# Gated DeltaNet and RWKV-7 step: the convolution's small PSUM copies on another engine, and the gate columns' transposes at another place

## The chip, the cores and the metric

The kernel runs on one core of one Trainium2 chip. The metric is the device time of one execution in microseconds (us); lower is better. The profile shows five engines: TensorE (PE for its matmuls, PEld for its weight loads), VectorE (DVE), ScalarE (ACT), GpSimd (POOL) and SyncE (SP), which issues the DMAs. Each engine works through its own queue in order; an instruction that waits for a semaphore holds up everything behind it on that engine, and nothing on the others.

## The reference

The program is one inference step of two layers, for 1040 prompt tokens (16 of them learned) and 8 samples of 8 tokens: 1104 tokens of width 1024. The first layer is a gated DeltaNet, and only it is touched:

```python
proj = xn @ w_in
qkv, z, b, a = proj[..., :c1], proj[..., c1:c2], proj[..., c2:c3], proj[..., c3:]
qkv, new_buf = causal_conv(qkv, conv_buf, conv_w)   # width 4, SiLU; new_buf: the last 3 rows before it
beta = jax.nn.sigmoid(b)
g = -jnp.exp(a_log) * jax.nn.softplus(a + dt_bias)  # then cumulative sums, exponentials, a triangular solve
```

There are 8 query/key heads and 16 value heads of 128 channels, hence 32 channel tiles (8 of queries, 8 of keys, 16 of values) that go through the convolution, and 16 tiles of output gates z that do not. The convolution begins with the last three rows of each sample's past (the history, an input), and the last three rows of each sequence are an output. The second layer is an RWKV-7 mixer, followed by a final norm.

## The kernel before

Tokens lie along the free dimension in three segments of 384, 384 and 336; the 64 sample tokens come first. A dense product of one 128-channel tile is 3 segments of 24 fp32 matmuls, since activations and weights are split into a high and a low part (`dense`, tile names d, dk, dq, dv, dz; ScalarE makes the high weights whi, GpSimd the low ones wlo).

`layer0` computes the two gates' rows first (`gates`): a dense product of the 32 gate channels, then on VectorE and ScalarE a chain of operations over 16 rows of 1104 tokens, which ends with the tile rows (lines 367 to 378). Rows are stored to DRAM (drow, line 389), and nine 128-token pieces of rows are transposed by TensorE into PSUM, three to a bank (lines 390 to 393). From there VectorE and ScalarE fill gcol, the same gates as columns with tokens on partitions (lines 396 to 399). gcol scales almost everything that follows.

Then come eight rounds of one key head and its two value heads. In each round: `gdn_keys` (convolution of the key tile), `gdn_prep` (scores of keys with keys, decay factors E read from drow, a masked exponential with a column of gcol as bias, and the inverse of the triangular blocks: 62 dependent VectorE operations invtmp and invT, lines 470 and 472, then a round through DRAM to the tiles T1n and TT), `gdn_queries`, `gdn_values` (two value tiles), `gdn_gate` (two tiles of z) and `gdn_recur`, the recurrence over nine token tiles, in which TensorE's rA products, ScalarE's w and VectorE's X and S alternate. In the first round `gdn_gate` comes ahead of `gdn_prep`.

`conv_tile` is the convolution of one tile and is called 32 times. For each it loads the history (24 rows of 128 channels), transposes it with TensorE (fhist), and copies the 24 columns from PSUM into the ends of the first segment's eight sample stretches (line 418, VectorE). ScalarE copies the dense products into raw (lines 420, 421, 426), scales by the first tap, VectorE adds three taps (cvy, line 434), ScalarE takes tanh, and VectorE multiplies (line 438). GpSimd collects the last three rows of each sequence in last. At the end TensorE transposes them (flast), VectorE copies 27 rows of 128 from PSUM to lasts (line 452), and two DMAs store them.

fhist, flast, the columns' transposes, the key scores and the values' transposes share two PSUM banks (tag f); the dense products of this layer use two others (tag d). In the first layer no order is written out by hand. The program text gives priorities and data dependences; from these a list scheduler, which goes by its own estimate of each instruction's time, draws up the queue of every engine when the program is built, and gives out the buffers as they come free in that estimate. So the order in the trace is not the order of the text, and a moved instruction can change the order of others. In the second layer the order on TensorE is written out by hand.

The views name a helper's line for some operations: line 73 is `transpose`, line 76 `mm`, line 62 `act`.

Of the kernel before, what the change touches and what calls it, by code (L numbers as in the profile page):

```python
# [35 lines left out]
class Builder:  # L36
# [307 lines left out]
    def gates(self, xh, xl):  # L344
        nc, i, t, gp = self.nc, self.i, self.t, self.gatep
        al, wz, rows, g, sm = self.gate_in
        nea = t(gp, [128, 1], "nea")
        self.act(nea[32:48], al[32:48, 0:1], AF.Exp)
        nc.vector.tensor_scalar(nea[32:48], nea[32:48], -1.0, None, op0=ALU.mult)
        whi = t(gp, [128, 8, 64], "whi2", dt=F32R)  # L350
        wlo = t(gp, [128, 8, 64], "wlo2", dt=F32R)
        self.split(wz, whi, wlo)
        w = ([whi[:, 0:4, :], whi[:, 4:8, :]], [wlo[:, 0:4, :], wlo[:, 4:8, :]])
        x = t(gp, [48, NT], "ax")
        y = t(gp, [48, NT], "ay")
        for s, (c0, n) in enumerate(SEGS):
            p = self.dense(w, 64, xh, xl, s)
            b = rows[0:16, c0:c0 + n]
            self.act(b, p[0:16, 0:n], AF.Tanh, scale=0.5)
            nc.vector.tensor_scalar(b, b, 0.5, 0.5, op0=ALU.mult, op1=ALU.add)  # L360
            xa, ya = x[32:48, c0:c0 + n], y[32:48, c0:c0 + n]
            self.act(xa, p[32:48, 0:n], AF.Identity, bias=al[32:48, 1:2])
            nc.vector.scalar_tensor_tensor(ya, xa, -1.0, xa, op0=ALU.mult, op1=ALU.max)
            self.act(ya, ya, AF.Exp, scale=-1.0)
        xa, ya = x[32:48], y[32:48]
        self.act(ya, ya, AF.Ln, bias=1.0)
        nc.vector.scalar_tensor_tensor(ya, xa, 0.0, ya, op0=ALU.max, op1=ALU.add)
        nc.vector.tensor_scalar(g[32:48, 0:NT], ya, nea[32:48], None, op0=ALU.mult)
        gc = rows[32:48]
        nc.vector.tensor_tensor_scan(gc, sm[32:48], g[32:48], 0.0, op0=ALU.mult, op1=ALU.add)  # L370
        gd = rows[64:80]
        c3 = lambda x: x.rearrange("p (c k) -> p c k", k=128)
        c8 = lambda x: x[:, 0:64].rearrange("p (c k) -> p c k", k=8)
        v, v8 = c3(gc), c8(gc)
        nc.vector.tensor_tensor(c3(gd)[:, 1:9], v[:, 1:9, 127:128].broadcast_to([16, 8, 128]), v[:, 1:9], op=ALU.subtract)
        nc.vector.tensor_tensor(c3(gd)[:, 0:1, 64:128], v[:, 0:1, 127:128].broadcast_to([16, 1, 64]), v[:, 0:1, 64:128],
                                op=ALU.subtract)
        nc.vector.tensor_tensor(c8(gd), v8[:, :, 7:8].broadcast_to([16, 8, 8]), v8, op=ALU.subtract)
        egl = t(gp, [48, 17], "egl")
        self.act(egl[32:48, 0:8].unsqueeze(2), v8[:, :, 7:8], AF.Exp)  # L380
        self.act(egl[32:48, 8:17].unsqueeze(2), v[:, :, 127:128], AF.Exp)
        dgl = self.dram([16, 17], "dgl")
        nc.sync.dma_start(dgl, egl[32:48])
        nc.sync.dma_start(self.eglb.rearrange("p h c -> p (h c)"),
                          dgl.rearrange("(o h) c -> o (h c)", o=1).broadcast_to([128, 272]))

        self.drow = self.dram([8, 9, 2, 128], "drow")
        for j in range(8):
            nc.sync.dma_start(self.drow[j].rearrange("t h k -> h t k"), c3(gc)[2 * j:2 * j + 2])
        for t3 in range(3):  # L390
            p = self.ps("f", 2)
            for k in range(3):
                self.transpose(p[:, 96 * k:96 * k + 96], rows[:, (3 * t3 + k) * 128:(3 * t3 + k + 1) * 128])
            pv = p[:, 0:288].rearrange("p (k x h) -> p k x h", k=3, h=16)
            c = self.col[:, 3 * t3:3 * t3 + 3]
            nc.vector.tensor_copy(c[:, :, 0, :], pv[:, :, 0, :])
            nc.vector.tensor_scalar(c[:, :, 1, :], pv[:, :, 2, :], -1.0, None, op0=ALU.mult)
            self.act(c[:, :, 2, :], pv[:, :, 2, :], AF.Exp)
            self.act(c[:, :, 3, :], pv[:, :, 4, :], AF.Exp)


    def conv_tile(self, ft, xh, xl, dst, done=None):

        nc, i, t = self.nc, self.i, self.t
        w, self.wnext = self.wnext or self.load_w(i["gdn_w_in"][0][:, ft * 128:(ft + 1) * 128]), None
        hist = t(self.fp, [24, 128], "hist", 1)
        nc.sync.dma_start(hist, i["state_gdn_conv"][0].rearrange("b r c -> (b r) c")[:, ft * 128:(ft + 1) * 128])
        last = t(self.fp, [128, 27], "last", 2)
        cw = [self.cw[:, k, ft:ft + 1] for k in range(4)]
        prev = None  # L410
        for s, (c0, n) in enumerate(SEGS):
            p = self.dense(w, 128, xh, xl, s, label="q" if ft < 8 else "k" if ft < 16 else "v")
            raw = t(self.fp, [128, 411], "raw", 3)
            if s == 0:
                sv = raw[:, 0:88].rearrange("p (b r) -> p b r", r=11)
                hp = self.ps("f", 2, "hist")
                self.transpose(hp[:, 0:24], hist)
                nc.vector.tensor_copy(sv[:, :, 0:3], hp[:, 0:24].rearrange("p (b r) -> p b r", r=3))
                nc.gpsimd.memset(raw[:, 88:91], 0.0)
                nc.scalar.copy(sv[:, :, 3:11], p[:, 0:64].rearrange("p (b r) -> p b r", r=8))  # L420
                nc.scalar.copy(raw[:, 91:411], p[:, 64:384])
                wd = 408
                nc.gpsimd.tensor_copy(last[:, 0:24].rearrange("p (b r) -> p b r", r=3), sv[:, :, 8:11])
            else:
                nc.gpsimd.tensor_copy(raw[:, 0:3], prev)
                nc.scalar.copy(raw[:, 3:3 + n], p[:, 0:n])
                wd = n
            prev = raw[:, wd:wd + 3]
            if s == 2:
                nc.gpsimd.tensor_copy(last[:, 24:27], prev)  # L430
            y = t(self.fp, [128, 408], "cvy", 2)
            self.act(y[:, 0:wd], raw[:, 0:wd], AF.Identity, scale=cw[0])
            for k in range(1, 4):
                nc.vector.scalar_tensor_tensor(y[:, 0:wd], raw[:, k:k + wd], cw[k], y[:, 0:wd], op0=ALU.mult, op1=ALU.add)  # L434
            e = raw
            self.act(e[:, 0:wd], y[:, 0:wd], AF.Tanh, scale=0.5)
            d = dst(s)
            silu = lambda d, e, y: nc.vector.scalar_tensor_tensor(d, e, 1.0, y, op0=ALU.add, op1=ALU.mult)
            if s == 0:
                v8 = lambda q: q[:, 0:88].rearrange("p (b r) -> p b r", r=11)[:, :, 0:8]  # L440
                silu(d[:, 0:64].rearrange("p (b r) -> p b r", r=8), v8(e), v8(y))
                silu(d[:, 64:384], e[:, 88:408], y[:, 88:408])
            else:
                silu(d[:, 0:n], e[:, 0:n], y[:, 0:n])
                if n < 384:
                    nc.gpsimd.memset(d[:, n:384], 0.0)
            if done is not None:
                done(s, d)
        lp = self.ps("f", 2, "last")
        self.transpose(lp[0:27, 0:128], last)  # L450
        ls = t(self.fp, [27, 128], "lasts", 1)
        nc.vector.tensor_copy(ls, lp[0:27, 0:128])
        nc.sync.dma_start(self.o["s_gdn_conv"][0].rearrange("b r c -> (b r) c")[:, ft * 128:(ft + 1) * 128], ls[0:24])
        nc.sync.dma_start(self.o["p_gdn_conv"][0, 0][:, ft * 128:(ft + 1) * 128], ls[24:27])

# [1365 lines left out]
    def layer0(self, top, right, xa, xc):  # L1821
        tc, nc, t = self.tc, self.nc, self.t
# [13 lines left out]
        self.vectors()  # L1836
        kh, kl = [h[:, k] for h in hi for k in range(4)], [l[:, k] for h in lo for l in h for k in range(l.shape[1])]
        rows = [xa[:, k] for k in range(6)] + [xc[:, k] for k in range(10)]
        self.gates(kh, kl)
        for j in range(8):  # L1840
            G, before = self.gdn_keys(j, kh, kl), G if j else None
            if j == 0:
                if QF:
                    self.gdn_queries(j, G, kh, kl)
                self.gdn_zero()
                gates.close()
                self.gp = pool("gdn", ctx)
                if ZF:
                    self.gdn_gate(j, G, kh, kl)
# [43 lines left out]
        lp = pool("rnorm", out, side="right")  # L1893
# [304 lines left out]
```

## Time and profile before

| | us |
|---|---|
| median of 3 runs | 2295.79 |
| lowest and highest | 2290.16, 2301.59 |
| the profiled execution | 2295.8 |
| its span | 2294.1 |
| TensorE, VectorE, ScalarE, GpSimd busy | 2133.1, 1558.2, 1273.9, 949.9 |

The span is the time from the first instruction to the last on the core; 1.7 us of the profiled execution lie around it. The rows of gates are made up to 67 us from the span's start, the eight rounds of the first layer run from about 45 to 1180 us, and the second layer fills the rest. In a timeline row stand the start, the time, engine, line, operation, the tile written and those read, and in brackets the time for which the engine had stood before and what released it. A waits row has the engine and tile that waited, the one waited for, the total in us, how often, and the longest. The granted clock (PEclk) is TensorE's clock as the throttle granted it, as a share of full speed.

### The profile page before, as it was taken

To read this page: it belongs to the slowest core of one execution; us is meant where nothing else is said; L and a number is where in the kernel's file an instruction comes from. 1 tells how busy PE (TensorE), PEld (TensorE's weight loads), DVE (VectorE), ACT (ScalarE), POOL (GpSimd) and SP (SyncE) were. 2 spreads that over 40 slices of the span, in tenths; PEclk is the share of its full clock that TensorE was granted. 3 is DMA by queue.
4 is the path that set the end of the run, shared out by engine and by line. 5 is a ranking of instruction groups with operands and counts; after the bars stand their busy time and mean duration, and the time that the engine had idled before them with its cause. 6 is when DMAs were issued, how large, how long until landed. Compare 5 with 4: busy or idle time off the path is not lost.

```text
span 2294.1 us, 55205 instructions
## 1 busy us (share of the span) xinstructions
PE 2133.1 (93%) x20452; PEld 1943.4 (85%) x20452; DVE 1558.2 (68%) x4200; ACT 1273.9 (56%) x3638; POOL 949.9 (41%) x1285
## 2 busy tenths in 40 slices
PE   6989999999999999999998999888899999999997
PEld 5887988889898898989898998777789888888786
DVE  6778769585867869586334776847866647766655
ACT  5445556465565556466533474654745446777674
POOL 3435344443433344453322351563724244444444
PEclk9999999999999999999999999899999999999999
DMA  4334332323333242335335225565454375677754
GB/s 116 96 82 109 79 92 74 102 84 84 111 90 95 66 114 69 103 96 165 113 100 150 69 63 193 176 189 161 143 168 126 102 218 155 182 220 220 226 166 135
DMA packets 430663, 292.67 MB, mean 128 GB/s; under 512 B 147145, under 2 KB 412986, under 8 KB 430394
## 3 DMA queue, kind: packets, MB, share of 16 engines
q1 hardware_dynamic: 430394, 289.14, 44.2%
q8 instruction: 161, 2.64, 0.5%
q14 instruction: 108, 0.88, 0.1%
HBM read 197.68 MB, written 91.37 MB: 126 GB/s over the span
## 4 chain that ended last, share of the span: by engine, by line
PE 53%; DVE 15%; DMA 9%; ACT 8%; POOL 5%; issue 5%; SPq 1%; DVEq 0%; POOLq 0%; ACTq 0%
PE d L76 16%; PE dz L76 6%; PE rA L76 4%; PE dk L76 4%; PE dq L76 3%; DVE invT L472 2%; DVE invtmp L470 2%; DMA attn<-drow 2%; PE rX L80 2%; DVE cvy L434 1%; PE do L76 1%; POOL attn L545 1%; DMA sldcak<-cakd 1%; PE fG L76 1%; PE zz L76 1%
## 5 line engine op out<-in xcount | busy, mean ns | idle before, releaser
L90 POOL TENSOR_TENSOR wlo<-wraw,whi 128x512 fp32r<-128x512 f32 (+1 forms) x246 | 325.2, 1325 | 364.4 <-ACT whi L86 346.8
L76 PE MATMUL d<-xc,whi 128*128 128x384 f32 (+2 forms) x1006 | 287.6, 343 | 4.0 <-ACT whi L86 2.1
L86 ACT CAST whi<-wraw 128x512 fp32r<-128x512 f32 (+1 forms) x246 | 150.2, 614 | 101.4 <-PE dq L76 50.7
L76 PEld LDWEIGHTS d<-xc,whi 128*128 128x128 f32 (+1 forms) x1006 | 186.6, 192 | 8.8 <-ACT whi L86 2.9
L434 DVE SCALAR_TENSOR_TENSOR cvy<-raw,cw,cvy 128x408 f32<-128x408 f32 (+2 forms) x288 | 178.4, 633 | 16.8 <-ACT cvy L62 14.9
L76 PE MATMUL d<-xc,wlo 128*128 128x384 f32 (+3 forms) x476 | 163.5, 347 | 6.8 <-POOL wlo L90 6.8
L76 PE MATMUL dz<-xc,whi 128*128 128x384 f32 (+1 forms) x480 | 149.9, 343 | 0.0
L76 PE MATMUL d<-xa,whi 128*128 128x384 f32 (+3 forms) x450 | 144.3, 345 | 2.8 <-ACT ev L2000 2.1
L76 PE MATMUL dv<-xc,whi 128*128 128x384 f32 (+1 forms) x480 | 146.7, 334 | 0.0
L834 POOL TENSOR_SCALAR Sb<-Sb,eglb 128x128 f32<-128x128 f32 x128 | 81.2, 652 | 89.0 <-DMA Sb<-in_state_gdn 45.1
L76 PE MATMUL dz<-xa,whi 128*128 128x384 f32 (+1 forms) x288 | 101.3, 352 | 0.0
L76 PEld LDWEIGHTS d<-xc,wlo 128*128 128x128 f32 (+1 forms) x476 | 91.3, 192 | 11.8 <-POOL wlo L90 7.8
L472 DVE TENSOR_TENSOR invT<-invT,invtmp 72x31 f32<-72x31 f32 (+15 forms) x248 | 99.0, 399 | 2.8
L470 DVE TENSOR_TENSOR invtmp<-invA,invT 72x31 f32<-72x31 f32 (+15 forms) x248 | 96.0, 387 | 7.2 <-DMA invA<-ltd 4.4
L76 PE MATMUL dv<-xa,whi 128*128 128x384 f32 (+1 forms) x288 | 100.1, 347 | 0.1
L76 PEld LDWEIGHTS d<-xa,whi 128*128 128x128 f32 (+1 forms) x450 | 85.4, 192 | 6.3 <-ACT ev L2000 2.4
L76 PEld LDWEIGHTS dz<-xc,whi 128*128 128x128 f32 x480 | 90.0, 193 | 0.8
L76 PEld LDWEIGHTS dv<-xc,whi 128*128 128x128 f32 x480 | 88.5, 188 | 0.5 <-issue 0.4
L1044 DVE SCALAR_TENSOR_TENSOR mixs<-xb,pcol,mixs 128x320 f32<-128x320 f32 (+2 forms) x96 | 78.3, 823 | 15.3 <-ACT mixs L62 14.6
L76 PE MATMUL d<-xa,wlo 128*128 128x384 f32 (+3 forms) x252 | 86.0, 341 | 1.5 <-POOL wlo L90 1.5
L62 ACT ACTIVATE o<-rA,gcol 128x128 f32<-128x128 f32 x128 | 46.7, 373 | 71.4 <-DVE S L745 70.9
L62 ACT ACTIVATE attn<-attn,gcol 128x128 f32<-128x128 f32 x144 | 46.6, 392 | 70.0 <-POOL attn L545 69.9
(521 smaller groups left out, 7061.8 us busy)
## 6 DMA issues: line engine op xcount, KB each, us to landing
wraw<-in_gdn_w_in SPq DMA_DIRECT2D x96, 256.0 KB
wraw<-in_rwkv_w_rkvz SPq DMA_DIRECT2D x80, 256.0 KB
Sb<-in_state_gdn SPq DMA_DIRECT2D x64, 256.0 KB
sldcak<-cakd SPq DMA_DIRECT2D x24, 576.0 KB
cakd<-ev SPq DMA_DIRECT2D x56, 192.0 KB
wraw<-in_rwkv_w_o SPq DMA_DIRECT2D x42, 256.0 KB
E<-drow SPq DMA_DIRECT2D x24, 384.0 KB
attn<-drow SPq DMA_DIRECT2D x24, 384.0 KB
```

Of the source, the lines that this page charges most:

```text
L62: return self.nc.scalar.activation(out, in_, func, bias=bias, scale=scale, **kw)
L76: self.nc.tensor.matmul(out, lhsT, rhs, start=start, stop=stop)
L80: self.nc.tensor.matmul(out, lhsT, rhs, start=start, stop=True, skip_group_check=True)
L86: nc.scalar.copy(hi, x)
L90: e.tensor_tensor(lo, x, hi.bitcast(F32), op=ALU.subtract)
L434: nc.vector.scalar_tensor_tensor(y[:, 0:wd], raw[:, k:k + wd], cw[k], y[:, 0:wd], op0=ALU.mult, op1=ALU.add)
L470: nc.vector.tensor_tensor(tmp, A[:, j, j + 1:32].unsqueeze(2).broadcast_to([nb, n, m]), Tv[:, j, 0:m].unsqueeze(1).broadcast_to([nb, n, m] ...
L472: nc.vector.tensor_tensor(Tv[:, j + 1:32, 0:m], Tv[:, j + 1:32, 0:m], tmp, op=ALU.subtract)
L545: nc.gpsimd.affine_select(E6, E6, pattern=[[0, 6], [1, 128]], compare_op=ALU.is_ge, fill=NEG, base=0, channel_multiplier=-1)
L834: nc.gpsimd.tensor_scalar(Sb[:, u], Sb[:, u], self.eglb[:, hv, 4 * g + u:4 * g + u + 1], None, op0=ALU.mult)
L1044: nc.vector.scalar_tensor_tensor(x[:, f:], xb[:, 8 + a + f:8 + b], mu, x[:, f:], op0=ALU.mult, op1=ALU.add)
```

## The change

The two copies from PSUM in `conv_tile` go to ScalarE: the history's (line 418, 24 columns of 128 partitions) and the last tokens' (line 452, 27 rows of 128). Each is made 32 times. And `gates` ends after the rows are stored; the transposes of rows and the filling of gcol become a function of their own, called behind the first key tile's convolution instead of ahead of it.

```diff
@@ gates
             nc.sync.dma_start(self.drow[j].rearrange("t h k -> h t k"), c3(gc)[2 * j:2 * j + 2])
+        return rows
+
+    def gates_columns(self, rows):
+        nc = self.nc
         for t3 in range(3):
             p = self.ps("f", 2)
@@ conv_tile
                 self.transpose(hp[:, 0:24], hist)
-                nc.vector.tensor_copy(sv[:, :, 0:3], hp[:, 0:24].rearrange("p (b r) -> p b r", r=3))
+                nc.scalar.copy(sv[:, :, 0:3], hp[:, 0:24].rearrange("p (b r) -> p b r", r=3))
@@
         ls = t(self.fp, [27, 128], "lasts", 1)
-        nc.vector.tensor_copy(ls, lp[0:27, 0:128])
+        nc.scalar.copy(ls, lp[0:27, 0:128])
@@ layer0
-        self.gates(kh, kl)
+        gate_rows = self.gates(kh, kl)
         for j in range(8):
             G, before = self.gdn_keys(j, kh, kl), G if j else None
             if j == 0:
+                self.gates_columns(gate_rows)
                 if QF:
                     self.gdn_queries(j, G, kh, kl)
```

QF is 0 in both kernels, so the two lines behind the call do nothing.

## The prediction

> **What bounds the kernel now.** I read the page first, then the waits of TensorE and of VectorE in the window 60 to 1060 us (the stage that holds every line of the change), then the timeline around the two kinds of wait that the change touches, and the granted clock by stretches.
>
> ```profile
> span 2294.1 us, 55205 instructions
> ...
> PE 2133.1 (93%) x20452; PEld 1943.4 (85%) x20452; DVE 1558.2 (68%) x4200; ACT 1273.9 (56%) x3638; POOL 949.9 (41%) x1285
> ...
> PE 53%; DVE 15%; DMA 9%; ACT 8%; POOL 5%; issue 5%; SPq 1%; DVEq 0%; POOLq 0%; ACTq 0%
> ```
> The same by stretches (busy us of PE, PEld, DVE, ACT, POOL, then granted clock, DMA share, GB/s):
> ```profile
> 60.00:1060.00 1000.00, 954.49 (x7848) 875.33 (x7847) 742.93 (x2166) 547.10 (x1724) 411.56 (x636) 0.98 0.34 92
> ```
> In the stage TensorE is busy 954 of 1000 us, VectorE 743, ScalarE 547. So whatever the change gains must come out of some 46 us in which TensorE stands, and out of stretches at half clock. An engine that is merely relieved gives nothing by itself.
>
> TensorE stands in two places that this diff names. The first is at the start (TensorE's timeline, with the idle time before a row and what ended it):
> ```profile
> 62.48 0.31 PE L76 MATMUL dk<-xc,whi 128*128 128x336 f32 x1
> 66.78 0.71 PE L73 MATMUL f<-ident,rows 96*128 96x96 f32 x6 [3.99 <-DVE rows L378]
> 68.06 0.74 PE L73 MATMUL f<-ident,rows 96*128 96x96 f32 x3 [0.57 <-ACT gcol L62]
> ...
> 68.97 0.69 PE L76 MATMUL dz<-xa,whi 128*128 128x384 f32 x1
> ```
> All 72 matmuls of the first key tile are done at 62.8. Next in TensorE's queue are the nine transposes of the gates' rows, and the rows are not ready until VectorE ends line 378 at 66.7. The next dense product (dz, the output gates) waits behind them. After the stop the clock is low, here in the first row, and it is so again later after shorter stops:
> ```profile
> 67.72:74.55 6.83, 6.49 (x21) 6.21 (x22) 4.97 (x13) 3.50 (x12) 2.31 (x7) 0.50 0.95 254
> 252.04:255.45 3.41, 3.41 (x12) 3.41 (x12) 3.41 (x13) 2.13 (x8) 0.00 (x0) 0.50 0.48 138
> 255.45:258.87 3.42, 3.42 (x22) 3.42 (x22) 2.33 (x7) 0.68 (x2) 0.00 (x0) 1.00 0.00 0
> ...
> 774.28:777.69 3.41, 3.41 (x13) 3.41 (x12) 3.41 (x12) 2.01 (x8) 0.00 (x0) 0.50 0.48 138
> ```
> At clock 0.50 a stretch of 3.4 us holds 12 matmuls, at 1.00 it holds 22. Half of a low stretch is therefore lost: 3.4 us of the 6.83, 1.7 us of each 3.41.
>
> The second place is the transpose of the convolution's history (fhist), which waits for the copy of last tokens (lasts):
> ```profile
> PE fhist L73 <- DVE lasts L452: 8.2, 7, 1.7
> ```
> ```profile
> DVE raw L418 <- PE fhist L73: 19.6, 7, 4.2
> ```
> ```profile
> 250.56 0.24 PE L73 MATMUL fhist<-ident,hist 24*128 24x24 f32 x1 [1.69 <-DVE lasts L452]
> ...
> 772.68 0.24 PE L73 MATMUL fhist<-ident,hist 24*128 24x24 f32 x1 [1.70 <-DVE lasts L452]
> ```
> Seven stops (us in total, times, longest) make 8.2 us on TensorE. The long ones are alike; of three, the first and the last are shown in its timeline, each ending some 1.5 us ahead of a low stretch, at 252 and 774 above.
>
> **The change part by part.**
>
> Part A, the columns (lines 390 to 399) given out behind the first keys' convolution. Nothing is added: nine transposes, six VectorE and six ScalarE instructions move, with no DMA among them; the writes of drow stay ahead. They move past the first key tile's instructions on four engines and past its history load and two stores on SP, none of which depends on them. What goes on TensorE: 3.99 + 0.57 us of waiting and 3.4 us of low clock, 8.0 us at most. TensorE would run dz at once, since ScalarE could empty the keys' banks (raw) when they are done, not behind the columns as now:
> ```profile
> 67.70 0.56 ACT L62 ACTIVATE gcol<-f 128x48 f32<-128x48 f32 x4 [3.46 <-DVE gcol L397]
> 68.14 0.83 ACT L426 COPY raw<-dk 128x384 f32<-128x384 f32 x2
> ```
> The two copies that free those banks sit behind an instruction that stood 3.46 us.
>
> What is late next? TensorE stands again at 144, for the solved triangular blocks of the first head pair, and that chain runs through VectorE:
> ```profile
> PE rY L76 <- DMA T1n<-g_t: 3.9, 1, 3.9
> ```
> ```profile
> 78.00:144.00 66.00, 63.75 (x442) 61.33 (x442) 56.55 (x157) 29.53 (x85) 26.37 (x41) 1.00 0.26 68
> ```
> So part A is worth no more than VectorE's chain gains, unless the next keys fill TensorE's wait. VectorE at the start:
> ```profile
> 58.55 1.30 DVE L367 SCALAR_TENSOR_TENSOR ay<-ax,ay 16x1104 f32<-16x1104 f32 x1 [3.49 <-ACT ay L62]
> ...
> 66.51 0.21 DVE L378 TENSOR_TENSOR rows<-rows 16x64 f32<-16x64 f32 x1
> 67.28 0.21 DVE L396 COPY gcol<-f 128x48 f32<-128x48 f32 x1 [0.56 <-PE f L73]
> 67.41 0.20 DVE L397 TENSOR_SCALAR gcol<-f 128x48 f32<-128x48 f32 x1
> ...
> 70.13 3.96 DVE L434 SCALAR_TENSOR_TENSOR cvy<-raw,cw,cvy 128x408 f32<-128x408 f32 x6 [0.87 <-ACT cvy L62]
> ```
> The convolution could begin at 66.7 instead of 70.1, 3.4 us earlier. The six column instructions come back later at the 0.13 us pitch of 67.28 to 67.41, 0.8 us: 2.6 us are left. The hole of 3.49 us ahead of 58.55 could take the first segment's three steps, half of the 3.96 us group: another 2.0, together 4.6. The ends of part A are 0 (all of it waits at 144 again) and 8.0. I take 5 us: VectorE's sum, and 0.4 for a pair of copies that leaves its queue before 144.
>
> If the cover fails, the columns arrive late. Their first readers are the exponentials of E, and these also wait for E's load and its mask on GpSimd:
> ```profile
> 72.56 1.12 POOL L545 TENSOR_SCALAR_AFFINE_SELECT E<-E 128x768 f32<-128x768 f32 x1 [3.34 <-DMA E<-drow]
> ```
> ```profile
> 69.26 0.31 ACT L62 ACTIVATE gcol<-f 128x48 f32<-128x48 f32 x2 [0.29 <-DVE raw L418]
> ```
> The first mask ends at 73.7 and the last column on ScalarE at 69.6, so there are some 4 us of slack; beyond them a delay goes into VectorE's chain one for one.
>
> Part B, both copies by ScalarE. The rows (forms: min/median/max ns) and ScalarE's nearest rows from PSUM:
> ```profile
> L418 DVE COPY raw<-fhist x32: 163/178/184, 69.1 to 1031.3; 128x24 f32<-128x24 f32 x32
> ```
> ```profile
> L452 DVE COPY lasts<-flast x32: 268/271/279, 76.0 to 1049.1; 27x128 f32<-27x128 f32 x32
> ```
> ```profile
> L817 ACT COPY sS<-fsr 64x256 f32<-64x256 f32 x16 | 5.9, 368 | 3.5 <-PE fsr L76 3.4
> ...
> L420 ACT COPY raw<-dv 128x64 f32<-128x64 f32 x16 | 3.2, 199 | 0.0
> ```
> VectorE loses 32 x (0.18 + 0.27) = 14.4 us. ScalarE gains 32 history copies of 24 elements, estimated 0.2 us from the 64-element row (between 0 and 0.2), and 32 copies of 128, estimated 0.25 us, between 0.2 and 0.37: 14 us together. It stands 453 us of the 1000, so the work itself I cost at nothing; without that cover it costs those 14.
>
> The ceiling of part B is 8.2 us of stops plus the three low stretches of 1.7 us, 13.3 us. Is it reached? What lies around the stop at 250.56, TensorE, then VectorE, then ScalarE:
> ```profile
> 251.84 0.64 PE L76 MATMUL rA<-S,K 128*128 128x128 f32 x2 [0.18 <-DVE S L745]
> ```
> ```profile
> 248.21 1.32 DVE L472 TENSOR_TENSOR invT<-invT,invtmp 72x207 f32<-72x207 f32 x1
> ...
> 250.23 0.27 DVE L452 COPY lasts<-flast 27x128 f32<-27x128 f32 x1
> ...
> 251.45 0.33 DVE L745 SCALAR_TENSOR_TENSOR S<-S,eglb,rA 128x128 f32<-128x128 f32 x1
> ```
> ```profile
> 251.82 0.37 ACT L62 ACTIVATE o<-rA,gcol 128x128 f32<-128x128 f32 x1 [2.90 <-DVE S L745]
> ```
> ScalarE stood 2.9 us up to 251.82, so it would make the copy at about 249 and fhist would start 1.4 us earlier. But four matmul pairs later TensorE needs S, which VectorE, late by the slow row at 248.21, writes at 251.45 in a queue without pauses. Of 1.69 us perhaps 0.3 comes back there, and the rest becomes a wait for S. The other view is VectorE's work as a whole: 15% of the span on the chain beside 68% busy, so some 22% of its work sets the end, and 22% of 14.4 us are 3.2 us. I take 4 us, near this sum, and keep 0 and 13.3 as ends.
>
> The trace's rows put a low stretch behind a 1.7 us stop. The Trainium skill (TensorE: Matmul & The Clock Gate, What's actually happening) says otherwise: the gate closes after a whole idle window of about 3.4 us. By that rule the three short stops have no part in the low clock, and removing them would give 8.2 us at most instead of 13.3. The rows show the low clock within 1.6 us of such stops, so I keep 13.3 as the end.
>
> Part C, added waits. The history copy on ScalarE waits for fhist as VectorE's did. Behind it in ScalarE's queue can stand the weight casts (whi), the scaling of w and the exponentials, on all of which TensorE waits. I cost it at 0 for the likeliest case, since ScalarE has idle time to take the wait, and price it among the rivals.
>
> Sum: 5 + 4 = 9 us. The profiled execution took 2295.8 us (2294.1 span and 1.7 around it), the median of the runs is 2295.79, so no correction: **2286.8 us**. All that follows 1060 us keeps its work and shifts.
>
> **The rivals.**
>
> *All of it is TensorE's* (chance 0.22). If the next dense products always fill what VectorE leaves open, both ceilings come in: 8.0 + 13.3 = 21.3 us, 2274.5. For it: TensorE is the bound in the stage and dense products depend on no state. Against: the 251.84 row, and the stop at 144.
>
> *The waits only change their names* (0.20). The first head pair's triangular blocks end with VectorE, TensorE stands 8 us more at 144, and S takes the place of lasts: 0 to 2 us gained, 2294 to 2296. This is also the case in which the change does not do what it says: the order of this stage is drawn up at build time by what is ready, so the transposes can land in the queue where they are. Against: 2.6 us of VectorE's gain need nothing but the removed wait.
>
> *ScalarE becomes the engine that stands* (0.13). Line 418's 19.6 us in seven stops, 2.8 us each, pass to ScalarE. Where a whi cast or a w is queued behind, TensorE stands for it, and a stop of that length brings 1.7 us of low clock: 4.5 us each. Five of seven are 22.5 us, against 9 gained: 2309. It decides from two stops on, where 9 us are eaten up. For it: w and whi are what TensorE needs next. Against: ScalarE has half its time free, and the longest of the seven, up to 4.2 us, is a wait that TensorE shares:
> ```profile
> 148.94 0.18 DVE L418 COPY raw<-fhist 128x24 f32<-128x24 f32 x1 [3.83 <-PE fhist L73]
> ```
> These 3.83 us lie in TensorE's own stop at 144.
>
> **How the numbers follow.** My forecast has 0.45 and by itself goes from 2280 to 2294 (part A 2 to 8, part B 0 to 8). From 0.5% on (11.5 us, about what a measurement of this kernel can tell from no change) are the times under 2284.3 and over 2307.3. Faster: 0.22 of the first rival and 0.15 of the forecast, 0.37. Slower: the larger part of the last rival, 0.1. Within: the rest, 0.53. For 8 in 10 the range takes in the first rival with a margin, and the last one up to its price: 2272 to 2309.
>
> **What would show it.** Right in part A: dz starts near 63, no stop of 4 us there, granted clock 1.00 at 68 to 74, and the first rY earlier than 148.4; by how much is part A's worth. Wrong: TensorE's wait for T1n at 144 grows by what was gained. Right in part B: fhist no longer waits for lasts and the low stretches behind it are gone; wrong: waits of rA for S or w grow by the same amount, or whi's and w's rows stand behind raw L418 on ScalarE. The prediction is wrong as a whole if the new order of the stage opens other stops: then the sum of TensorE's waits between 60 and 1060 us tells it, 46 us now.

## The result and the profile after

| | median us | runs | lowest and highest |
|---|---|---|---|
| before | 2294.94 | 22 | 2286.84, 2305.03 |
| after | 2303.36 | 22 | 2292.45, 2310.49 |

The ratio is 1.0032, with a 95% interval of 1.0019 to 1.0045: the changed kernel is slower, by 8.4 us between the medians, by some 7 us by the ratio. (A ratio here isn't quite that of the two medians; the two ways differ by up to 3 us, here and below.) That is inside the range (2272 to 2309) and inside the half per cent that was called no change, but it lies on the other side of the start than the forecast (2286.8). The profiled execution of after took 2310.49 us, the slowest of its 22, at a mean granted clock of 0.968; that of before ran at 0.973. So differences between single profiles count for less here than those between medians.

The page of after, the span with the engines' busy time and the shares of the chain that ended last:

```profile
span 2308.8 us, 55212 instructions
...
PE 2150.9 (93%) x20452; PEld 1955.9 (85%) x20452; DVE 1558.1 (67%) x4136; ACT 1289.1 (56%) x3702; POOL 953.6 (41%) x1285
...
PE 59%; DVE 14%; DMA 9%; ACT 7%; POOL 4%; issue 4%; SPq 1%; DVEq 0%; POOLq 0%; ACTq 0%
```

64 instructions have gone from VectorE to ScalarE, as the diff says, but VectorE's busy time over the span has not fallen (1558.2 before). TensorE's share of the chain rose from 53% to 59%.

The stage of the change in after, by stretches (busy us and count of PE, PEld, DVE, ACT, POOL, granted clock, DMA share, GB/s):

```profile
60.00:1060.00 1000.00, 958.00 (x7624) 875.68 (x7623) 739.76 (x2087) 556.07 (x1773) 411.75 (x631) 0.97 0.34 90
62.80:66.80 4.00, 3.21 (x20) 2.89 (x18) 3.94 (x3) 1.61 (x5) 3.07 (x1) 1.00 0.00 1
67.72:74.55 6.83, 6.74 (x41) 5.94 (x40) 6.12 (x12) 1.64 (x4) 2.94 (x5) 1.00 0.18 46
```

The last two rows are the place of part A's stop. TensorE is busy 3.21 of the 4 us in which it stood before, and the clock from 67.7 to 74.5 is 1.00 where it was 0.50. Its timeline there in after:

```profile
63.58 0.33 PE L76 MATMUL dz<-xa,whi 128*128 128x384 f32 x1
...
67.08 0.44 PE L76 MATMUL dz<-xc,wlo 128*128 128x384 f32 x1 [1.06 <-POOL wlo L90]
...
75.15 0.47 PE L73 MATMUL f<-ident,rows 96*128 96x96 f32 x3 [0.69 <-ACT gcol L62]
...
87.75 0.44 PE L76 MATMUL dz<-xc,wlo 128*128 128x384 f32 x1 [2.67 <-POOL wlo L90]
...
146.19 0.37 PE L76 MATMUL rY<-T1n,E 32*32 32x32 f32 x6 [2.13 <-DMA T1n<-g_t]
```

dz now starts at once, and the columns' transposes come among its matmuls. But dz soon waits for its own low weights (1.06 and 2.67 us), and the first rY is 2.2 us earlier (148.36 before).

TensorE's waits from 60 to 1060 us (total us, times, longest), first of after, then the two rows of before that match its first two and have not been shown:

```profile
PE rA L76 <- DVE S L749: 15.1, 13, 2.0
PE rA L76 <- DVE o L757: 5.0, 10, 1.1
PE dz L76 <- POOL wlo L90: 3.7, 2, 2.7
...
PE rY L76 <- DMA T1n<-g_t: 2.7, 2, 2.1
```

```profile
PE rA L76 <- DVE S L745: 9.5, 16, 2.2
...
PE rA L76 <- DVE o L753: 0.6, 3, 0.2
```

The 8.2 us of fhist behind lasts are gone from the list, and the waits for S and o have together grown by 10.0 us. Still, all of TensorE's standing in these 1000 us has shrunk: 1000 less 954.5 before, 1000 less 958.0 after, 45.5 and 42.0 us. By that sum alone the changed kernel should be faster. The same row says why the sum deceives: in an equal stretch TensorE made 224 matmuls fewer (x7624 for x7848). Busy time isn't progress. The rounds show progress better. Each row below is from the start of a key product dk to that of the next: all up to the third round, one round, then four, then the last and its tail, first before, then after:

```profile
0.00:290.40 290.40, 250.29 (x1987) 228.75 (x1987) 217.45 (x559) 152.35 (x417) 117.34 (x189) 0.97 0.36 97
290.40:421.00 130.60, 126.41 (x1029) 115.63 (x1029) 93.86 (x281) 71.09 (x229) 51.91 (x82) 0.97 0.34 89
421.00:939.20 518.20, 499.95 (x4106) 457.56 (x4106) 378.74 (x1120) 288.35 (x921) 212.61 (x329) 0.99 0.34 92
939.20:1174.10 234.90, 225.35 (x1700) 209.03 (x1701) 136.59 (x384) 127.78 (x447) 88.81 (x122) 1.00 0.39 109
```

```profile
0.00:290.70 290.70, 250.38 (x1951) 227.59 (x1951) 218.78 (x543) 152.68 (x424) 114.98 (x184) 0.96 0.34 93
290.70:429.30 138.60, 134.94 (x1069) 121.50 (x1067) 95.20 (x273) 78.98 (x258) 54.92 (x87) 0.95 0.34 93
429.30:950.10 520.80, 504.44 (x4099) 461.09 (x4099) 379.03 (x1088) 294.22 (x944) 217.14 (x329) 0.98 0.34 91
950.10:1189.90 239.80, 230.18 (x1712) 212.77 (x1711) 135.90 (x379) 128.59 (x450) 87.78 (x120) 0.99 0.37 106
```

Both kernels start the third round's dk at 290 us (290.4 and 290.7). After that the changed kernel loses 8.0 us in one round, 2.6 in the next four, 4.9 in the last and its tail: 15.5 us, while what follows the rounds is 1.1 us shorter (1120.0 and 1118.9 us). The loss shows far behind the columns, in rounds in which no line but the two copies is changed. Part of the 8.0 us was owed before, though. Up to 290 us the changed kernel has made 36 matmuls fewer (x1951 for x1987): 36 products rU of 64 x 64 that before makes ahead of dk come behind it in after, where they take 4.4 us:

```profile
291.90 1.54 PE L76 MATMUL rU<-TT,invA 64*64 64x64 f32 x12
...
294.62 2.82 PE L76 MATMUL rU<-TT,invA 64*64 64x64 f32 x24
```

Both rows lie in a stretch of 10.2 us at half clock. From the third round's dk to the end of the rounds, TensorE is at half clock for 20.5 us in before's profile and for 37.3 us in after's. If half of such a stretch is lost, as the prediction worked out, that makes some 8 of the 15.5 us in these two profiles.

And the two copies on ScalarE, its waits in the same stretch and the operations themselves (ns: lowest, median, highest):

```profile
ACT lasts L456 <- PE flast L73: 24.8, 15, 2.5
...
ACT raw L422 <- PE fhist L73: 7.7, 10, 1.8
```

```profile
L456 ACT COPY lasts<-flast x32: 238/253/257, 71.8 to 1059.6; 27x128 f32<-27x128 f32 x32
```

```profile
L422 ACT COPY raw<-fhist x32: 158/184/200, 55.7 to 1040.4; 128x24 f32<-128x24 f32 x32
```

The durations are as estimated (0.25 and 0.2 us). ScalarE now stands 32.5 us for the two transposes. That looked like the third rival come true, and was the first suspect.

### The profile page after: what moved, and what is told of

Read it like the earlier page. It is cut to its first block, busy times and chain, and to the rows that moved or that the text cites. A ratio compares the mean times of both kernels' runs of the same rounds, so it can differ in the third digit from the quotient of the medians.

```text
span 2308.8 us, 55212 instructions
## 1 busy us (share of the span) xinstructions
PE 2150.9 (93%) x20452; PEld 1955.9 (85%) x20452; DVE 1558.1 (67%) x4136; ACT 1289.1 (56%) x3702; POOL 953.6 (41%) x1285
## 4 chain that ended last, share of the span: by engine, by line
PE 59%; DVE 14%; DMA 9%; ACT 7%; POOL 4%; issue 4%; SPq 1%; DVEq 0%; POOLq 0%; ACTq 0%
PE d L76 16%; PE dz L76 7%; PE rA L76 5%; PE dk L76 4%; PE dq L76 4%; PE dv L76 3%; DMA attn<-drow 2%; PE rX L80 2%; DVE invT L476 2%; PE do L76 2%; DMA sldcak<-cakd 2%; DVE invtmp L474 2%; PE fG L76 1%; DVE cvy L438 1%; PE rU L76 1%
## 5 line engine op out<-in xcount | busy, mean ns | idle before, releaser
L62 ACT ACTIVATE mixs<-xb,omu 128x64 f32<-128x64 f32 (+3 forms) x128 | 62.4, 520 | 22.6 <-POOL xa L90 5.9
```

The source lines that it names most:

```text
L62: return self.nc.scalar.activation(out, in_, func, bias=bias, scale=scale, **kw)
```

## The experiments

**Two theories for the loss.** S: ScalarE's queue pays; a waiting copy holds up what TensorE needs next. By S each copy costs something by itself, both cost the sum, and the columns are innocent. O: the edits themselves are harmless or good, but any edit of the text makes the list scheduler draw other queues for the whole first layer, and the drawn order costs. By O a kernel without any work moved can lose as much, and the change with the queues held as before must gain.

All ratios are against runs of before on the same chip, with a 95% interval. The work is the same in every kernel.

**The parts alone.** From after, with both copies on VectorE again:

```diff
-                nc.scalar.copy(sv[:, :, 0:3], hp[:, 0:24].rearrange("p (b r) -> p b r", r=3))
+                nc.vector.tensor_copy(sv[:, :, 0:3], hp[:, 0:24].rearrange("p (b r) -> p b r", r=3))
-        nc.scalar.copy(ls, lp[0:27, 0:128])
+        nc.vector.tensor_copy(ls, lp[0:27, 0:128])
```

> Only the columns' transposes move; both copies stay on VectorE. Theory O (the loss comes from the order of the first layer's queues, drawn up anew, and shows as low clock and not as stops): the 4 us stop at 62.8 us is gone, what it gave is back in use by 150 us, and the time is within 8 us of before, either sign, with the fhist stops for lasts still there. Theory S (the copies on ScalarE cost the time, the columns gain): 3 to 6 us faster than before.

Measured: 0.9989 (0.9970 to 1.0009). The columns alone make no difference that shows. From before, with both copies on ScalarE:

```diff
-                nc.vector.tensor_copy(sv[:, :, 0:3], ...)
+                nc.scalar.copy(sv[:, :, 0:3], ...)
-        nc.vector.tensor_copy(ls, lp[0:27, 0:128])
+        nc.scalar.copy(ls, lp[0:27, 0:128])
```

> Only the two copies go to ScalarE; the columns stay ahead of the first keys. Theory S: 11 to 14 us slower than before, since ScalarE's waits for fhist and flast are all there and the columns' gain is not. Theory O: its time is that of another drawing of the same queues, within 10 us of before, and its difference and that of the columns alone do not add up to the 8 us of the whole change.

Measured: 1.0029 (1.0009 to 1.0048). The loss comes with the copies. Then each of them alone, first the last tokens' (the second pair of lines above), then the history's (the first pair):

> Only the last tokens' copy goes to ScalarE. Theory S: most of the loss, 6 to 10 us, since ScalarE's waits for flast were 25 us in the changed kernel against 8 for fhist. Theory O: no fhist stops of 1.7 us, waits of rA for S in their place, and a time within 8 us of before.

Measured: 1.0064 (1.0042 to 1.0086).

> Only the history's copy goes to ScalarE. Theory S: a small loss, 0 to 4 us. Theory O: the stops of fhist for lasts stay, because lasts stays with VectorE, and the time is within 8 us of before, either sign.

Measured: 1.0071 (1.0047 to 1.0095). By the ratios, one copy costs more than twice what both cost together. Costs that sit in ScalarE's queue, as S has them, would add up, to 1.0135 here; S can't give this. O's own sizes were missed as well: it had each within 8 us of before, and they are 15 and 16 us off. In e4 the operation that moved is the history's, and yet what grew in TensorE's waits is this:

```profile
PE fhist L73 <- DVE lasts L452: 14.3, 7, 2.4
PE rA L76 <- DVE o L753: 8.0, 11, 1.5
```

Both name VectorE (8.2 and 0.6 before).

**Rewriting without moving work.** Four kernels in which only the text's order of independent lines differs. The first is before with the history's copy, still on VectorE, written behind ScalarE's two raw copies:

```diff
-                nc.vector.tensor_copy(sv[:, :, 0:3], ...)
                 nc.gpsimd.memset(raw[:, 88:91], 0.0)
                 nc.scalar.copy(sv[:, :, 3:11], ...)
                 nc.scalar.copy(raw[:, 91:411], p[:, 64:384])
+                nc.vector.tensor_copy(sv[:, :, 0:3], ...)
```

> The kernel before, with the history's copy left on VectorE and only written two lines further down, behind ScalarE's copies of the dense product: no operation changes its engine, size or operands. Theory O (a redrawn order of the first layer's queues is what costs): 5 to 16 us slower than before, like the two single copies, with longer low clock in the last rounds. Theory S (a copy on ScalarE costs through ScalarE's queue): within 4 us of before.

Measured: 1.0134 (1.0103 to 1.0165). The second is before with the last tokens' transpose, copy and stores written ahead of what follows the last segment (the moved lines stand here as one comment):

```diff
+            if s == 2:
+                # transpose of last, lasts, two stores
             if done is not None:
                 done(s, d)
```

> The kernel before, with the last tokens' transpose, copy and stores written ahead of the last segment's transposes of the values; both copies on VectorE, the work the same. Theory O: differs from before by several us, more likely slower (3 to 16 us). Theory S: within 4 us of before.

Measured: 1.0090 (1.0064 to 1.0115). The third is after, with its ScalarE copy of the history moved as in the first:

> The changed kernel, with the history's copy on ScalarE written behind ScalarE's copies of the dense product instead of ahead of them. Theory O: as far from the changed kernel (8 us over before) as any redraw, anything from 0 to 16 us over before. Theory S: ScalarE no longer stands for fhist ahead of the copies that empty TensorE's banks, so faster than the changed kernel by some of its 7.7 us of waiting for fhist: 0 to 4 us over before.

Measured: 1.0167 (1.0141 to 1.0193). The fourth is before, with a call that the change doesn't touch at all:

```diff
-            self.gdn_sample_read(j, G)
             self.gdn_values(j, G, kh, kl)
+            self.gdn_sample_read(j, G)
```

> The kernel before, with the reading of the samples' states written behind the values' convolution instead of ahead of it; nothing of the change is in it and the work is the same. Theory O: several us from before, more likely slower (3 to 16 us). Theory S says nothing of it; if it and the two other rewritten kernels stay within 4 us of before, theory O has fallen.

Measured: 1.0165 (1.0135 to 1.0194). So a rewriting that moves no work to another engine loses 0.9 to 1.7%, more than the whole change did, and more than O had forecast (16 us at most; by the ratios they are 21 to 38 us off). The same stretch in e5 and then in e8:

```profile
60.00:1060.00 1000.00, 941.44 (x7552) 864.52 (x7550) 746.39 (x2126) 539.51 (x1692) 407.75 (x627) 0.97 0.33 89
```

```profile
60.00:1060.00 1000.00, 941.94 (x7458) 864.61 (x7458) 734.64 (x2112) 534.47 (x1689) 416.24 (x617) 0.96 0.33 88
```

296 and 390 matmuls fewer than before in the same 1000 us. Here part of it does show as standing (58.6 and 58.1 us, for 45.5).

**The order held.** The positive test of O: the edit is made, and every other instruction keeps the place that it has in its engine's queue in before. For this the program, once written, gets one dependence more per instruction, on its predecessor in the recorded queue. It concerns the issue order alone and adds no wait between engines. The moved instructions are left out and go where the scheduler puts them:

```diff
+        for names in recorded_queues.values():       # one list per engine
+            prev = None
+            for i in (here[n] for n in names if n in here):
+                if prev is not None:
+                    tc.add_manual_dep(i, prev.name, mybir.DependencyInfo(
+                        mybir.DependencyClass.NoSync, mybir.DependencyReason.DATA))
+                prev = i
```

In the traces, without the moved instructions, VectorE, ScalarE and GpSimd run in f1, f2 and f3 in the order of before, instruction for instruction; in after 1459 of VectorE's 4130 places hold another instruction than in before. The columns moved, all the rest held as before:

> Only the columns move, and every other instruction of every engine is held in the order that it has in the kernel before; the columns' 21 instructions go where the scheduler puts them. Theory O (the redrawn order is the loss): the 4 us stop at 62.8 us is gone and the time is 0 to 8 us below before. Theory S (ScalarE's copies are the loss): the same, it says nothing against it; if this is slower than before, the move itself costs.

Measured: 0.9998 (0.9977 to 1.0019). The copies on ScalarE, all the rest held:

> Only the two copies go to ScalarE, and all other instructions are held in the order of the kernel before; the 64 copies go where the scheduler puts them in ScalarE's queue. Theory O: the seven fhist stops for lasts go, nothing else moves, 0 to 13 us below before. Theory S: slower than before by about the 7 us of the two copies with a free order, since ScalarE's queue and its waits are the same.

Measured: 0.9980 (0.9962 to 0.9997). The whole change, all the rest held:

> The whole change, with all other instructions held in the order of the kernel before. Theory O: 2 to 21 us below before, about the sum of the two parts held, and so 10 us or more below the change with a free order. Theory S: at or above before.

Measured: **0.9968** (0.9947 to 0.9988); the medians are 2288.78 us for 2294.68. And the reverse, to see that the hold isn't itself what gains: the copies stay on VectorE, and the rest is held in the order that the changed kernel has:

> The counterpart: columns moved, both copies on VectorE, and all other instructions held in the order of the changed kernel; the 64 copies go where the scheduler puts them in VectorE's queue. Theory O: as slow as the changed kernel or slower (6 to 16 us over before), although no copy is on ScalarE. Theory S: as fast as the columns alone, 0 to 4 us below before.

Measured: 1.0056 (1.0035 to 1.0078). The order of after without its copies on ScalarE loses; the copies without that order gain. S has fallen, O stands. (A redrawing can also give tiles other buffers; what the order alone does and what the buffers do was not told apart.) What f3 looks like, its span and its rounds (cut as those above):

```profile
span 2274.4 us, 55206 instructions
```

```profile
288.10:415.00 126.90, 123.59 (x1029) 113.17 (x1029) 91.84 (x272) 71.78 (x237) 52.42 (x81) 1.00 0.34 90
415.00:927.50 512.50, 495.11 (x4105) 453.63 (x4106) 375.04 (x1088) 293.06 (x953) 211.98 (x329) 1.00 0.35 92
927.50:1160.50 233.00, 225.46 (x1701) 209.28 (x1701) 135.90 (x377) 129.20 (x456) 88.87 (x123) 1.00 0.38 110
...
60.00:1060.00 1000.00, 957.71 (x7958) 878.91 (x7957) 740.14 (x2113) 565.35 (x1813) 418.55 (x649) 0.99 0.35 94
```

The stage's TensorE busy time is that of after (957.7 and 958.0 us), with 334 matmuls more in it, and each of the rounds is shorter than in before. This profile is of f3's fastest execution and that of after of its slowest, so the two differ by 34.4 us in span where the medians differ by 14.6; f3's rounds have only 3.4 us at half clock.

**Which engine's order it is.** Two more theories: P, that TensorE's order alone decides, and D, that VectorE's does. The whole change, with only TensorE's queue held as before, then only VectorE's, then only the other three (ScalarE's, GpSimd's and SP's); the code is that of f3, with fewer lists:

> The whole change, with TensorE's queue alone held in the order of the kernel before. Theory P (the order on TensorE, the bound, is what counts): as fast as with every queue held, 3 to 11 us below before. Theory D (VectorE's order counts, since TensorE's stops end at VectorE): between the changed kernel and before, 0 to 8 us over before.

Measured: 0.9997 (0.9983 to 1.0011).

> The whole change, with VectorE's queue alone held in the order of the kernel before. Theory D: 3 to 11 us below before. Theory P: 3 to 12 us over before, as the changed kernel.

Measured: 0.9995 (0.9983 to 1.0007).

> The whole change, with the queues of ScalarE, GpSimd and SP held in the order of the kernel before, those of TensorE and VectorE free. Theories P and D: 3 to 12 us over before. Should it be as fast as with all held, the order of the casts and loads of weights is what counts.

Measured: 1.0100 (1.0078 to 1.0121). Neither P nor D: either queue brings back about half of the way from 1.0032 to 0.9968, and the other three queues held alone make it worse than leaving all free. No single queue decides; that it is how the queues fit together is the reading that is left, and it wasn't tried further.

## Why the prediction was wrong

**The step that failed** is the sum, 5 + 4 = 9 us. It costed both edits on the queues that the trace of before shows, and it has no term for the other instructions of the first layer: that all their queues are drawn anew was put at nothing, without a reason. The description of the kernel and the prediction both said that the order is drawn up at build time, and the prediction's last paragraph named "other stops" as what would make it wrong as a whole. But no rival had that mechanism, with a price and a chance; the rival on waits that change names used it only for where the transposes land. The runs put the size on it: the change at the order of before is 0.9968, the change as drawn 1.0032, so the redrawing costs 0.0064, about 15 us, and turns a gain of 7 into a loss of 7. Redrawings for other reasons cost 0.9 to 1.7%. What the prediction said of the rest, "All that follows 1060 us keeps its work and shifts", holds for what follows the rounds (1120.0 and 1118.9 us); the last round, which runs on past 1060 us, still loses.

**The check it set itself misled.** The sum of TensorE's waits between 60 and 1060 us was to tell such a case. It went the other way, 45.5 to 42.0 us, while the kernel became slower. What tells it is the time from one round's dk to the next, with a count of the matmuls made by then.

**Part B, the copies: size right at a held order, mechanism in part.** Forecast 4 us, measured 0.0020 x 2295 = 4.6 us (0.7 to 8.7); an interval this wide would have borne out most of the forecast's own 0 to 8, so the close hit is partly luck. Also as forecast, most of the 8.2 us came back as a wait for S. TensorE's waits in f2:

```profile
PE rA L76 <- DVE S L745: 15.7, 16, 1.9
...
PE fhist L73 <- ACT lasts L452: 1.5, 3, 0.5
```

fhist behind lasts went from 8.2 to 1.5, S from 9.5 to 15.7: of 6.7 us, 0.5 are left. The gain of 4.6 is more than that difference, and where the rest of it shows wasn't settled. The sign that the low stretches behind these stops would be gone did not come as a whole: f2's profile is at clock 0.50 for 3.4 us from 254.05 and from 516.88, and at 1.00 only around 774.

**Part A, the columns: mechanism seen, size too large.** Forecast 5 us; at a held order 0.0002 x 2295 = 0.5 us (a gain of 5.3 to a loss of 4.4), and 0.0012 x 2295 = 2.8 us as the difference of f3 and f2, which lies within the noise of both. The stop of 3.99 us goes, but in f1's TensorE timeline two others stand in its place:

```profile
63.62 0.46 PE L76 MATMUL dz<-xa,whi 128*128 128x384 f32 x1 [1.74 <-ACT raw L430]
...
76.81 2.29 PE L76 MATMUL fsc<-K 128*128 128x128 f32 x10 [2.12 <-ACT gcol L62]
...
147.42 0.52 PE L76 MATMUL rY<-T1n,E 32*32 32x32 f32 x6 [3.92 <-DMA T1n<-g_t]
```

1.74 us for the keys' bank, which ScalarE still had to empty, and 2.12 us behind ScalarE's copies of the columns. fsc multiplies K with K and reads no column; it shares the two banks of tag f with the columns' transposes, so it waits for a bank that these copies had yet to free. The prediction gave the columns' readers a cover of 4 us and did not speak of the bank. Nor did the low clock go: behind the two stops f1 has as much of it as before had behind its one (6.83 us).

```profile
63.91:67.32 3.41, 3.41 (x12) 3.41 (x12) 2.62 (x6) 1.14 (x2) 1.95 (x4) 0.50 0.31 66
77.56:80.97 3.41, 3.33 (x14) 3.09 (x13) 1.20 (x7) 3.41 (x14) 2.17 (x5) 0.50 0.23 88
```

The first rY comes 0.9 us earlier (148.36 before), not 4.6, behind the same wait of 3.9 us. For this part, the rival in which the waits only change their names described what happened.

**Part C, the added waits on ScalarE: cost 0, right.** They came, 32.5 us of them in after and 25.6 in f2; but f2, with the same work on ScalarE, is faster than before. An engine with over 40% of its time free took them. No run bears out the rival in which ScalarE becomes the engine that stands. One reason against it was misread, though: the 3.83 us at 148.94 are the fourth longest of line 418's waits, and in the three of 4.2 us, which end at 295.47, 559.38 and 817.70, TensorE was busy throughout and shared none of the wait.

**The mean clock is a smaller part of the 8.4 us.** Over its 22 runs after has a mean granted clock of 0.9724; before has 0.9737 over the 31 runs beside e1 to e4 and 0.9729 over the 34 beside f1 to f4. Within after's runs the time falls by some 1500 us per 1.0 of clock, so 0.0005 to 0.0013 are 1 to 2 us of the 8.4. In f3 (0.9744) it is 2 of the 5.9 us gained against the runs beside it, and in f4 (0.9723) 1 of about 13 lost, so an order can cost with hardly any change of clock. In e3 to e8 the clock weighs more: their means are 0.9665 to 0.9700, by the same slope an estimated 6 to 11 us of the 15 to 38 that they lose.

**What stays open.** How the redrawn order loses the time: no one wait carries it. Half clock in the rounds carries part of it in the profiles (from the third round's dk on 20.5 us in before, 37.3 in after, 58.0 in e5, 54.6 in e8), but each kernel has one profile, and how much of this belongs to the order and how much to the one execution isn't known. Also why the order drawn from the text of before is better than nearly all others tried: of nine freely drawn orders (after and e1 to e8), eight are slower and one can't be told from it. That is what was found, not explained.

## What to carry to other kernels

Where a scheduler draws the queues from the text, an edit has two effects: that of the moved work, and that of all queues being drawn anew; the second can be larger than the first, so price it from the spread of harmless rewritings (here 0.9 to 1.7%, and nothing that shows where only the columns moved) before trusting a sum of a few us. To judge an edit, hold the rest of the queues in their recorded order; here that also made the version that beats both kernels. And compare progress, not busy shares: the time from one round's first product to the next round's, and whether the same work lies between them.

## What the runs showed of the hardware

Half clock without a stop. In after the granted clock is 0.50 for 10.2 us from 290.45 on, and TensorE is busy throughout; in the window before it, too, it is busy 2.53 of 3.42 us. Windows of after:

```profile
287.03:290.45 3.42, 2.53 (x30) 2.07 (x29) 3.08 (x7) 1.97 (x6) 1.26 (x1) 1.00 0.16 57
290.45:293.86 3.41, 3.41 (x20) 2.81 (x19) 0.84 (x2) 1.87 (x5) 0.14 (x1) 0.50 0.92 225
293.86:297.27 3.41, 3.41 (x27) 2.96 (x26) 0.00 (x0) 2.15 (x7) 3.41 (x7) 0.50 0.55 204
297.27:300.69 3.42, 3.42 (x15) 3.32 (x14) 0.96 (x1) 1.98 (x7) 1.56 (x3) 0.50 0.24 69
```

```profile
288.24 0.91 PE L76 MATMUL rY<-T1n,E 64*64 64x64 f32 x12 [0.73 <-DVE T1n L649]
...
294.62 2.82 PE L76 MATMUL rU<-TT,invA 64*64 64x64 f32 x24
```

The longest stop in the 10 us ahead is the 0.73 us shown; what else lies there are runs of small matmuls, of 64 x 64 and 32 x 32. The Trainium skill (TensorE: Matmul & The Clock Gate, What's actually happening) lets the gate close after a whole idle window of about 3.4 us. This trace disagrees, as the 1.7 us stops of before did. Whether the small matmuls have a part in it wasn't tried; alone they are not enough, since f3 makes the same products between 270 and 300 us at a clock of 1.00.

The spread of one kernel is wide: 18 us between the lowest and the highest of 22 runs, both for before and for after, and in after it goes with the mean granted clock of the run (correlation -0.84). Differences of 0.2 to 0.3% took the medians of a dozen runs and more; those of 0.9% and more showed in 4 to 6.
